# Logits of two softmax maps as six products in alternating row halves of TensorE, and the values' product in another PSUM bank

## The chip, the cores and the metric

The kernel runs on one core of one Trainium2 chip. The metric is device time in microseconds (us) of one launch, the median of several runs. Lower is better. A run's time is slightly longer than the span of its profile, which goes from the first to the last recorded instruction.

## The reference

A trunk of two layers over 1024 tokens of width 1024, in float32. Layer 0 mixes tokens with a gated MLP and a gated delta rule, layer 1 with differential attention. Each layer also has an MLP and a gated projection. The change lies in the attention of layer 1 alone, cut here to what matters:

```python
# 8 heads; q and k have two maps (r) of 64 columns per head, v has 128
q = rms_norm(q.reshape(1, 1024, 8, 2, 64), q_gain) * 64 ** -0.5
k = rms_norm(k.reshape(1, 1024, 8, 2, 64), k_gain)
# for each block of 128 query rows
logits = einsum('bqhrd,bkhrd->bhrqk', q_blk, k) - slopes * dist     # causal
probs = softmax(logits)
attn = probs[:, :, 0] - lam * probs[:, :, 1]
o = einsum('bhqk,bkhe->bqhe', attn, v)
```

Each logit is a sum over 64 numbers, and each head needs it for two maps.

## The kernel before

**Numbers as pairs.** Large products run in a rounded float32 format that streams faster. An operand is kept as a rounded high part and a low part that holds what rounding took away. A product of two such operands is high*high + high*low + low*high: three products added up in one PSUM bank (`mm3`, line 206).

**Logits.** For each head, `begin` (line 956) makes the keys' operand `ks`. For map r it is a tile of 128 partitions: the 64 partitions of the map's own half hold the high part of k, and the other 64 hold the low part. `put_k` transposes four tiles of k on TensorE into a PSUM tile with the tag `tr`, and per map one ScalarE instruction (L969) writes the high part and one VectorE instruction (L970) the low part. `put_q` does the same for two blocks of queries: `qh` has the high part of q in both halves (ScalarE L980, then a copy by VectorE, L981), and `ql` has the low part in the map's own half and zeros in the other (L982). So one product of 128 rows, `qh` against `ks`, gives high*high + high*low at once, and a second one, `ql` against `ks`, gives low*high. The logits of one map and one chunk of up to 512 keys are two products of 128 rows.

**A block's steps.** There are 64 blocks: 8 heads by 8 blocks of 128 queries. Block b sees (b+1)*128 keys, in one chunk (b below 4) or two. For each map and chunk `logits` runs the two products into a PSUM bank (tags `aux` and `sc`, in turns `aux, sc, aux`). VectorE then adds the distance term, writes the result to `lg` and keeps the running minimum (L1016). ScalarE takes the exponential and its sum (L1019). `combine` subtracts map 1 from map 0 (VectorE, L1025 to L1027). `transpose` turns the result with TensorE into `tr` banks, which ScalarE copies out (L1037). `value` multiplies by v into a bank with the tag `sc` (`po`), which VectorE (L1047) and ScalarE (L1049) read. Map 0 has three `lg` buffers, map 1 only one.

**PSUM.** There are eight banks: the tags `mm`, `tr`, `aux` and `sc`, with two buffers each.

**Order.** The loop over g at the end of `attention` writes the steps of three blocks interleaved: map 0's logits of block g, `combine` of g-1, `transpose` of g-2, map 1's logits of g, `value` of g-2. Between them `pump` issues filling work: the projections to q, k and v of later heads (`mm<-w,hi`, `mm<-w,lo`), and from the last heads on the output projection (`mm<-ohi,w`) with its transposes (`put_o`, L1073, L1074). A scheduler then fixes the order on each engine. An engine executes its own list in that order and waits where an operand or a buffer isn't ready. `Ordered` (line 44) wraps TensorE's calls; its `floor` puts an instruction behind a named one in that order without making the engine wait for it.

Of the kernel before, what the change touches and what calls it, by code (L numbers as in the profile page):

```python
# [12 lines left out]
F32R = mybir.dt.float32r  # L13
AF = mybir.ActivationFunctionType
ALU = mybir.AluOpType
# [3 lines left out]
P = 128  # L19
# [4 lines left out]
HT = 512  # L24
# [3 lines left out]
AHEAD = 7  # L28
WB = 12
EARLY = 3000  # L30
LAG = 3
KA = (6, 5)
MARKS = ((64, 50), (192, 144), (223, 168))
# [6 lines left out]
def f32(ap):  # L40
    return ap.bitcast(F32)
# [73 lines left out]
class Trunk:  # L115
# [756 lines left out]
    def attention(self, w_qkv, w_out, gain_next, h_dram):  # L872

        nc = self.nc
        NB = NT
        hs, r = list(self.hs), list(self.r)
# [75 lines left out]
        qk_tag = itertools.cycle(("aux", "sc", "aux"))  # L952
        aT_tag = itertools.cycle(("c8", "c9", "c10"))
        heads = {}

        def begin(hd):

            qk = qks[hd]

            ks = self.slot(f"A{2 + hd % 2}", [P, 2, S], F32R, "ks")  # L960

            def put_k(hf):
                pt = self.aux([P, HT], "tr", "tr")
                for t in range(4):
                    self.pe.transpose(pt[:, t * P : (t + 1) * P], qk[1][hf][:, t, :], self.ident)
                for r in range(2):
                    own, other = half[r], half[1 - r]
                    dst = ks[:, r, hf * HT : (hf + 1) * HT]
                    nc.scalar.activation(dst[own], pt[own], AF.Copy, scale=self.kg[own])  # L969
                    nc.vector.scalar_tensor_tensor(dst[other], pt[own], self.kg[own], f32(dst[own]), ALU.mult, ALU.subtract)  # L970

            def put_q(b2):
                pt = self.aux([P, HT], "tr", "tr")
                for i in range(2):
                    self.pe.transpose(pt[:, i * P : (i + 1) * P], qk[0][b2 // 2][:, 2 * (b2 % 2) + i, :], self.ident)
                qh = self.slot(f"c{11 + b2 % 2}", [P, 2, 2 * P], F32R, "qh")
                ql = qlow[b2 % 2]
                for r in range(2):
                    own, other = half[r], half[1 - r]
                    nc.scalar.activation(qh[own, r], pt[own, 0 : 2 * P], AF.Copy, scale=self.qg[own])  # L980
                    nc.vector.tensor_copy(qh[other, r], f32(qh[own, r]))  # L981
                    nc.vector.scalar_tensor_tensor(ql[own, r], pt[own, 0 : 2 * P], self.qg[own], f32(qh[own, r]), ALU.mult, ALU.subtract)  # L982
                return qh, ql

            put_k(0)
            heads[hd] = [ks, put_k, put_q, put_q(0)]

        class Block:
# [13 lines left out]
            def logits(me, r):  # L1002
                hd, b, n, nm, lg = me.hd, me.b, me.n, me.nm, me.lg[r]
                if b == 0 and r == 0:
                    nc.vector.tensor_scalar(al, al, 0.5, None, ALU.mult)
                ks, _, _, (qh, ql) = heads[hd][:4]
                qs = slice((b % 2) * P, (b % 2 + 1) * P)
                nch = (n + HT - 1) // HT
                u0 = (NB - 1 - b) * P
                for c in range(nch):  # L1010
                    k0, k1 = c * HT, min(n, (c + 1) * HT)
                    ps = self.aux([P, HT], next(qk_tag), "qk")
                    self.pe.matmul(ps[:, : k1 - k0], lhsT=qh[:, r, qs], rhs=ks[:, r, k0:k1], start=True, stop=False)
                    self.pe.matmul(ps[:, : k1 - k0], lhsT=ql[:, r, qs], rhs=ks[:, r, k0:k1], start=False, stop=True)

                    nc.vector.tensor_tensor_reduce(  # L1016
                        out=lg[:, k0:k1], in0=ps[:, : k1 - k0], in1=al[:, u0 + k0 : u0 + k1], scale=-1.0,
                        scalar=3.0e38 if c == 0 else nm[:, r, 0:1], op0=ALU.add, op1=ALU.min, accum_out=nm[:, r, c : c + 1])
                nc.scalar.activation(lg[:, :n], lg[:, :n], AF.Exp, bias=nm[:, r, nch - 1 : nch], scale=-1.0, accum_out=me.sums[:, b, r : r + 1])  # L1019

            def combine(me):
                b, n, sums = me.b, me.n, me.sums
# [16 lines left out]
            def value(me):  # L1039
                hd, b = me.hd, me.b  # L1040
                if b % 4 == 0:
                    os[hd].append(self.slot(f"c{6 + b // 4}", [P, 4, P], F32, "o"))
                o, v = os[hd], vs[hd // 2]
                po = self.aux([P, P], "sc", "po")
                for k in range(b + 1):
                    self.pe.matmul(po, lhsT=me.aT[k // 4][:, (k % 4) * P : (k % 4 + 1) * P], rhs=v[:, k, (hd % 2) * P : (hd % 2 + 1) * P], start=k == 0, stop=k == b)
                nc.vector.tensor_copy(o[b // 4][:, b % 4, :], po)  # L1047
                sq = self.tmp(P)
                nc.scalar.activation(sq, po, AF.Square, accum_out=me.osq[:, b : b + 1])  # L1049
# [81 lines left out]
        tail = tails()  # L1131
        blocks = []
        for g in range(8 * NB + 2):
            if g < 8 * NB:
                hd, b = divmod(g, NB)
                blocks.append(Block(hd, b))
                blocks[g].logits(0)
            if 0 < g <= 8 * NB:
                blocks[g - 1].combine()
            pump()  # L1140
            if g < 8 * NB and b % 2 and b < NB - 1:
                q = heads[hd][2]((b + 1) // 2)
            if g > 1:
                blocks[g - 2].transpose()
            pump()
            if g < 8 * NB:
                if b == 3 - (hd < 7):
                    heads[hd][1](1)
# [834 lines left out]
```

## Time and profile before

| | us |
|---|---|
| median of 3 runs | 2536.91 |
| lowest and highest run | 2536.68, 2537.27 |
| span of the profiled execution | 2535.2 |
| median run less that span (start and end around it) | 1.7 |
| attention's blocks: first to last logits product on TensorE | 1270.7 to 1720.4 |

Of the profiled execution the span is what is recorded; no separate run time stands beside it. In the profile PE is TensorE's products, PEld its weight loads, DVE VectorE, ACT ScalarE, POOL GpSimd. A TensorE row gives the start, the duration and the shape: `128*128` is rows by columns of the array in use, `128x512` is partitions by columns streamed. Successive products overlap, so a product's cost to TensorE is read from start to start and not from its duration. In merged timeline rows `x8` means that eight instructions start one after another, and the duration goes from the first start to the last end. A plain float32 product is recorded as two passes, a transpose or a rounded product as one.

### The profile page before, as it was taken

The page shows a single profiled execution, that of the slowest core. Times are in us where ns is not written, and L with a number is a line of the kernel's source. Part 1 is how long each engine was busy: PE and PEld are TensorE (multiplying, and loading weights), DVE is VectorE, ACT ScalarE, POOL GpSimd, SP SyncE. Part 2 cuts the span into 40 slices and gives each one's busy share as a digit, 9 for nine tenths or more (in the row PEclk, how much of TensorE's full clock was granted, in tenths as well). Part 3 has the DMA queues.
Part 4 walks back from the last instruction along what each step waited for, and adds up shares of the span by engine and source line. Part 5 has one row for each costly group of instructions (what it writes and reads, how often), then busy time and mean ns, then how long its engine had stood idle before and what let it go on. Part 6 is the DMA issues. An engine that isn't in the chain of part 4 may idle for free.

```text
span 2535.2 us, 40147 instructions
## 1 busy us (share of the span) xinstructions
PE 2515.3 (99%) x14046; PEld 2151.9 (85%) x14046; DVE 1854.3 (73%) x3676; ACT 1285.9 (51%) x2553; POOL 285.5 (11%) x256
## 2 busy tenths in 40 slices
PE   9999999999999999999999999999999999999999
PEld 7898898888888878888999999988778888888877
DVE  7867776697666888656477777787887677787586
ACT  6543444465455434544366666665654555445452
POOL 0301232000000000000334333310000000000000
PEclk9999999999999999999999999999999999999999
DMA  7452435457557756553211111147466558655651
GB/s 242 126 157 78 136 110 193 138 175 242 161 174 257 245 164 207 183 158 120 74 53 47 55 47 43 59 136 257 143 219 202 174 184 281 216 184 185 200 178 59
DMA packets 298818, 396.92 MB, mean 157 GB/s; under 512 B 37780, under 2 KB 165752, under 8 KB 298616
## 3 DMA queue, kind: packets, MB, share of 16 engines
q1 hardware_dynamic: 298600, 394.36, 48.4%
q8 instruction: 110, 1.80, 0.3%
q14 instruction: 92, 0.75, 0.1%
q10 hardware_dynamic: 16, 0.00, 0.0%
HBM read 289.40 MB, written 104.86 MB: 156 GB/s over the span
## 4 chain that ended last, share of the span: by engine, by line
PE 92%; DVE 4%; DMA 2%; issue 1%; ACT 1%; SPq 0%; POOL 0%; DVEq 0%; ACTq 0%; POOLq 0%
PE mm L76 79%; PE po L76 3%; PE qk L76 2%; PE aux L76 2%; PE tr L79 2%; DMA raw<-in_w_ple_gate_dram 1%; DVE lg L1016 0%; DVE w L224 0%; DMA raw<-in_w_mlp_dram 0%; PE pz L76 0%; PE py L76 0%; PE aux L79 0%; PE pvn L76 0%; PE pab L79 0%; PE pkq L76 0%
## 5 line engine op out<-in xcount | busy, mean ns | idle before, releaser
L76 PE MATMUL mm<-g,w 128*128 128x512 f32 x2592 | 603.6, 394 | 0.8 <-DVE g L224 0.5
L223 ACT CAST w<-raw 128x512 fp32r<-128x512 f32 x598 | 366.0, 618 | 453.8 <-PE mm L76 386.8
L76 PEld LDWEIGHTS mm<-g,w 128*128 128x128 f32 x2592 | 485.9, 188 | 116.2 <-DVE g L224 1.0
L76 PE MATMUL mm<-hi,w 128*128 128x512 f32 x1728 | 553.6, 396 | 0.3 <-ACT hi L1219 0.3
L76 PE MATMUL mm<-w,hi 128*128 128x256 f32 (+2 forms) x2528 | 505.5, 295 | 0.0
L224 DVE TENSOR_TENSOR w<-raw,w 128x512 fp32r<-128x512 f32 x534 | 364.8, 690 | 178.9 <-ACT w L223 169.4
L76 PEld LDWEIGHTS mm<-w,hi 128*128 128x128 f32 x2528 | 400.1, 188 | 13.6 <-DVE acc L284 0.3
L76 PEld LDWEIGHTS mm<-hi,w 128*128 128x128 f32 x1728 | 324.7, 188 | 73.7 <-ACT hi L1219 0.7
L76 PE MATMUL mm<-w,lo 128*128 128x256 f32 (+2 forms) x1264 | 370.3, 293 | 0.0
L76 PE MATMUL mm<-lo,w 128*128 128x512 f32 x864 | 341.6, 396 | 0.9 <-DVE lo L1220 0.9
L76 PE MATMUL mm<-t,w 128*128 128x512 f32 x1152 | 270.9, 394 | 1.2 <-ACT w L223 1.2
L76 PEld LDWEIGHTS mm<-t,w 128*128 128x128 f32 x1152 | 216.2, 188 | 52.8 <-ACT w L223 1.6
L76 PEld LDWEIGHTS mm<-w,lo 128*128 128x128 f32 x1264 | 238.2, 188 | 5.6
L76 PEld LDWEIGHTS mm<-lo,w 128*128 128x128 f32 x864 | 162.8, 188 | 36.8 <-DVE lo L1220 1.4
L224 DVE TENSOR_TENSOR g<-graw,g 128x512 fp32r<-128x512 f32 x216 | 147.2, 685 | 8.8 <-DMA gd<-g 6.9
L223 ACT CAST g<-graw 128x512 fp32r<-128x512 f32 x216 | 132.7, 617 | 32.8 <-issue 10.9
L1019 ACT ACTIVATE lg<-lg,nm 128x128 f32<-128x128 f32 (+7 forms) x128 | 99.5, 777 | 82.5 <-DVE nm L1016 76.0
L260 POOL TENSOR_TENSOR r<-ms,mhalf 128x4 f32<-128x4 f32 x12 | 13.3, 1109 | 1060.9 <-DVE ms L258 1033.5
L350 ACT ACTIVATE g<-g 128x512 f32<-128x512 f32 x96 | 60.6, 632 | 114.8 <-DVE g L284 114.5
L1016 DVE CUSTOM_DVE_ANT_0 lg<-qk,al 128x512 f32<-128x512 f32 (+3 forms) x128 | 75.1, 589 | 36.2 <-PE qk L76 32.8
L224 POOL TENSOR_TENSOR w<-raw,w 128x512 fp32r<-128x512 f32 x64 | 84.6, 1347 | 111.9 <-ACT w L223 63.0
L76 PE MATMUL mm<-ohi,w 128*128 128x512 f32 x256 | 85.2, 400 | 0.5 <-ACT ohi L1073 0.5
(336 smaller groups left out, 3612.4 us busy)
## 6 DMA issues: line engine op xcount, KB each, us to landing
raw<-in_w_mlp_dram SPq DMA_DIRECT2D x352, 256.0 KB, 3.3
graw<-gd SPq DMA_DIRECT2D x224, 256.0 KB, 2.8
gd<-g SPq DMA_DIRECT2D x192, 256.0 KB, 3.1
raw<-in_w_ple_gate_dram SPq DMA_DIRECT2D x76, 256.0 KB, 3.5
acc<-h_dram SPq DMA_DIRECT2D x64, 256.0 KB, 4.4
keep<-in_w_mlp_dram SPq DMA_DIRECT2D x64, 256.0 KB, 4.3
raw<-in_w_in_e_dram SPq DMA_DIRECT2D x60, 256.0 KB, 3.7
h_dram<-acc SPq DMA_DIRECT2D x48, 256.0 KB, 2.5
```

The source lines that it names most:

```text
L76: self._next(self.engine.matmul(*a, **k))
L79: self._next(self.engine.transpose(*a, **k))
L223: self.nc.scalar.copy(hi, src)
L224: (lo_engine or self.nc.vector).tensor_tensor(lo, src, f32(hi), ALU.subtract)
L260: nc.gpsimd.tensor_tensor(r, ms, self.mhalf[:, 0:4], ALU.pow)
L350: nc.scalar.activation(g, src, AF.Relu)
L1016: nc.vector.tensor_tensor_reduce(out=lg[:, k0:k1], in0=ps[:, : k1 - k0], in1=al[:, u0 + k0 : u0 + k1], scale=-1.0, scalar=3.0e38 if c == 0 ...
L1019: nc.scalar.activation(lg[:, :n], lg[:, :n], AF.Exp, bias=nm[:, r, nch - 1 : nch], scale=-1.0, accum_out=me.sums[:, b, r : r + 1])
```

## The change

The keys' operand `ks` becomes two tiles of 128 partitions, high and low, with map 0 in partitions 0 to 63 and map 1 in 64 to 127; the queries' operand has the same form. One ScalarE and one VectorE instruction over 128 partitions make each of them, where `put_k` had two and two and `put_q` two and four. The logits of both maps for one chunk are now made together: three products for each map, each of 64 rows and 128 columns, in the order map 0, map 1, map 0, map 1 and so on. Map 0 uses the array's upper 64 rows and writes an `aux` bank, map 1 the lower 64 rows and an `sc` bank. Each of the six is put behind the one before in TensorE's order, the first behind the exponential of an earlier chunk, and the scheduler gets a higher priority for them. `po` moves from `sc` to `tr`. In the loop `combine` of block g-1 now stands ahead of block g's logits, and both maps' logits stand together.

```diff
+AT_ONCE = 200
...
-        qlow = [self.slot(t, [P, 2, 2 * P], F32R, "ql") for t in ("c13", "d0")]
-        for t in qlow:
-            nc.vector.memset(f32(t), 0.0)
...
-                for r in range(2):
-                    own, other = half[r], half[1 - r]
-                    dst = ks[:, r, hf * HT : (hf + 1) * HT]
-                    nc.scalar.activation(dst[own], pt[own], AF.Copy, scale=self.kg[own])
-                    nc.vector.scalar_tensor_tensor(dst[other], pt[own], self.kg[own], f32(dst[own]), ALU.mult, ALU.subtract)
+                hi, lo = (ks[:, i, hf * HT : (hf + 1) * HT] for i in range(2))
+                nc.scalar.activation(hi, pt, AF.Copy, scale=self.kg)
+                nc.vector.scalar_tensor_tensor(lo, pt, self.kg, f32(hi), ALU.mult, ALU.subtract)
...
-                for r in range(2):
-                    own, other = half[r], half[1 - r]
-                    nc.scalar.activation(qh[own, r], pt[own, 0 : 2 * P], AF.Copy, scale=self.qg[own])
-                    nc.vector.tensor_copy(qh[other, r], f32(qh[own, r]))
-                    nc.vector.scalar_tensor_tensor(ql[own, r], pt[own, 0 : 2 * P], self.qg[own], f32(qh[own, r]), ALU.mult, ALU.subtract)
-                return qh, ql
+                q = self.slot(f"c{11 + b2 % 2}", [P, 2, 2 * P], F32R, "qs")
+                nc.scalar.activation(q[:, 0], pt[:, 0 : 2 * P], AF.Copy, scale=self.qg)
+                nc.vector.scalar_tensor_tensor(q[:, 1], pt[:, 0 : 2 * P], self.qg, f32(q[:, 0]), ALU.mult, ALU.subtract)
+                return q
...
-                    ps = self.aux([P, HT], next(qk_tag), "qk")
-                    self.pe.matmul(ps[:, : k1 - k0], lhsT=qh[:, r, qs], rhs=ks[:, r, k0:k1], start=True, stop=False)
-                    self.pe.matmul(ps[:, : k1 - k0], lhsT=ql[:, r, qs], rhs=ks[:, r, k0:k1], start=False, stop=True)
...
+                    pss = [self.aux([P, HT], t, "qk") for t in ("aux", "sc")]
+                    if len(scaled) > 1:
+                        self.pe.floor = scaled[-2]
+                    with self.tc.high_priority(AT_ONCE):
+                        for i, (x, y) in enumerate(((0, 0), (0, 1), (1, 0))):
+                            for r in range(2):
+                                self.pe.matmul(pss[r][:, : k1 - k0], lhsT=q[half[r], x, qs], rhs=ks[half[r], y, k0:k1], start=i == 0, stop=i == 2)
+                                self.pe.floor = self.pe.mark
+                    self.pe.floor = None
...
-                po = self.aux([P, P], "sc", "po")
+                po = self.aux([P, P], "tr", "po")
...
+            if 0 < g <= 8 * NB:
+                blocks[g - 1].combine()
             if g < 8 * NB:
                 hd, b = divmod(g, NB)
                 blocks.append(Block(hd, b))
-                blocks[g].logits(0)
-            if 0 < g <= 8 * NB:
-                blocks[g - 1].combine()
+                blocks[g].logits()
...
-                blocks[g].logits(1)
```

More of the change, by code (lines that the diff above doesn't have):

```diff
@@ L951, in attention @@
         lg1 = lgs[1][:, 1]
-        qk_tag = itertools.cycle(("aux", "sc", "aux"))
+        scaled = []
         aT_tag = itertools.cycle(("c8", "c9", "c10"))
@@ L1011, in logits @@
                     k0, k1 = c * HT, min(n, (c + 1) * HT)
-                    ps = self.aux([P, HT], next(qk_tag), "qk")
-                    self.pe.matmul(ps[:, : k1 - k0], lhsT=qh[:, r, qs], rhs=ks[:, r, k0:k1], start=True, stop=False)
-                    self.pe.matmul(ps[:, : k1 - k0], lhsT=ql[:, r, qs], rhs=ks[:, r, k0:k1], start=False, stop=True)
[L1016 to L1019, printed above, removed]
+                    pss = [self.aux([P, HT], t, "qk") for t in ("aux", "sc")]
[7 more added lines that the diff above has]
+                    self.pe.floor = None
+                    scaled.append(None)
+                    for r in range(2):
+                        nc.vector.tensor_tensor_reduce(
+                            out=lg[r][:, k0:k1], in0=pss[r][:, : k1 - k0], in1=al[:, u0 + k0 : u0 + k1], scale=-1.0,
+                            scalar=3.0e38 if c == 0 else nm[:, r, 0:1], op0=ALU.add, op1=ALU.min, accum_out=nm[:, r, c : c + 1])
+                for r in range(2):
+                    inst = nc.scalar.activation(lg[r][:, :n], lg[r][:, :n], AF.Exp, bias=nm[:, r, nch - 1 : nch], scale=-1.0, accum_out=me.sums[:, b, r : r + 1])
+                scaled[-nch:] = [inst.ins.name] * nch
             def combine(me):
```

15 lines of the change are left out of this document (6 added, 9 removed).

## The prediction

> **What bounds the kernel now.** First the page: span, busy time by engine, and the chain of work that ended last.
>
> ```profile
> span 2535.2 us, 40147 instructions
> PE 2515.3 (99%) x14046; PEld 2151.9 (85%) x14046; DVE 1854.3 (73%) x3676; ACT 1285.9 (51%) x2553; POOL 285.5 (11%) x256
> PE 92%; DVE 4%; DMA 2%; issue 1%; ACT 1%; SPq 0%; POOL 0%; DVEq 0%; ACTq 0%; POOLq 0%
> ```
>
> TensorE is busy for 99% of the span and carries 92% of the chain. As a busy TensorE need not be one at its peak, I look at the stage that changes: the windows of the attention, then what TensorE waited for in 1260 to 1760 us (total, times, longest).
>
> ```profile
> 1300.00:1400.00 100.00, 99.03 (x803) 96.72 (x802) 72.80 (x212) 62.08 (x153) 40.63 (x35) 1.00 0.17 51
> 1500.00:1600.00 100.00, 100.00 (x810) 97.89 (x810) 74.05 (x221) 61.41 (x153) 36.52 (x32) 1.00 0.14 43
> 1655.00:1720.00 65.00, 62.98 (x370) 53.65 (x369) 54.40 (x143) 40.52 (x95) 7.36 (x7) 1.00 0.47 153
> PE tr L79 <- DVE olo L1074: 1.8, 3, 0.7
> PE qk L76 <- DVE nm L1016: 1.5, 2, 0.8
> PE mm L76 <- ACT ohi L1073: 0.5, 1, 0.5
> PE po L76 <- ACT aT L1037: 0.4, 2, 0.2
> PE tr L79 <- ACT aT L1037: 0.2, 1, 0.2
> ```
>
> Of each 100 us TensorE (first pair after the length) is busy 99 to 100, VectorE (third) some 73, and the granted clock (the 1.00) is full. All waits of TensorE in these 500 us add up to 4.4 us. So the stage lasts as long as TensorE's own stream of products; only near 1655 to 1720 does VectorE, 54.4 of 65, come close. The change is worth what it does to that stream.
>
> **The products: three rounds for four.** The logits' products by tile, and their pace from the timeline:
>
> ```profile
> L76 PE MATMUL qk<-ks,qh x192: 219/392/483, 1270.7 to 1720.2; 128*128 128x512 f32 x96, 128*128 128x128 f32 x32, 128*128 128x256 f32 x32, 128*128 128x384 f32 x32
> L76 PE MATMUL qk<-ks,ql x192: 221/388/477, 1270.8 to 1720.4; 128*128 128x512 f32 x96, 128*128 128x128 f32 x32, 128*128 128x256 f32 x32, 128*128 128x384 f32 x32
> ...
> 1350.62 0.40 PE L76 MATMUL qk<-ks,qh 128*128 128x512 f32 x1
> 1350.85 0.39 PE L76 MATMUL qk<-ks,ql 128*128 128x512 f32 x1
> 1351.08 0.40 PE L76 MATMUL mm<-w,hi 128*128 128x256 f32 x2
> ...
> 1354.45 0.28 PE L76 MATMUL qk<-ks,qh 128*128 128x256 f32 x1
> 1354.57 0.28 PE L76 MATMUL qk<-ks,ql 128*128 128x256 f32 x1
> ...
> 1499.95 1.05 PE L76 MATMUL po<-v,aT 128*128 128x128 f32 x8
> ```
>
> From start to start 512 columns take 0.23 us and 256 take 0.12. For 384 I take the middle, 0.175. Eight passes of 128 columns start over 1.05 - 0.27 us, so 0.11 each: there the weight load of 128 columns sets the pace. I price a logits product of 128 columns at 0.11 too.
>
> Both maps of a chunk make a pair: 48 pairs of 512 columns (half of 96) and 16 each of 384, 256 and 128. One product per pair over all of them is 48 x 0.23 + 16 x (0.175 + 0.12 + 0.11) = 17.5 us. Before, a pair is four products one after another, 70 us in all. After, it is six in two halves of the array. If the halves run side by side these are three rounds, 52.5 us: **17.5 us saved**. That they run side by side is bounded by the nearest row, the delta rule's 32-row products, which go to different parts of the array:
>
> ```profile
> 200.10 0.45 PE L76 MATMUL pz<-inv 32*32 32x32 f32 x24
> 205.63 0.40 PE L76 MATMUL mm<-hi,w 128*128 128x512 f32 x1
> 205.96 0.67 PE L76 MATMUL py<-xt,am 64*64 64x64 f32 x8
> 206.57 0.51 PE L76 MATMUL mm<-hi,w 128*128 128x512 f32 x1
> 206.91 0.38 PE L76 MATMUL po<-state,qkv 128*128 128x128 f32 x2
> ...
> 205.96 0.54 PEld L76 LDWEIGHTS py<-xt,am 64*64 64x64 f32 x8 [0.36 <-issue]
> 206.56 0.19 PEld L76 LDWEIGHTS mm<-hi,w 128*128 128x128 f32 x1
> ...
> L76 PE MATMUL py<-xt,am x64: 218/218/267, 206.0 to 375.8; 64*64 64x64 f32 x64
> ...
> 4.27 0.18 PEld L79 LDWEIGHTS aux<-ident,t 8*128 8x128 f32 x1 [0.33 <-issue]
> 4.47 0.59 PEld L79 LDWEIGHTS aux<-ident,x 128*128 128x128 f32 x5
> ```
>
> 24 products of 32 columns last 0.45 us, the last one some 0.19 of it, so they start 0.011 apart. The 64-column ones, all in one part of the array, start (0.67 - 0.22)/7 = 0.064 apart, which would be 0.03 for 32 columns. So three parts do run side by side, loads included. No row shows two halves that share all 128 columns; that is the first rival.
>
> **The switch between array shapes.** The same rows show its price. The 512-column product at 205.63 would let the next start at 205.86; the first 64-row one starts at 205.96: 0.10 lost. Its load can't be made ahead: the first `py` lasts 267 ns instead of 218, 0.05 for 64 columns, so by the pace above 0.11 for 128. On the way back the last `py` starts at 205.96 + 0.67 - 0.22 = 206.41 and is paced out at 206.475, but the next load starts at 206.56: 0.09. That product's successor starts 0.34 after it instead of 0.23: 0.11 for its exposed load. Together **0.41 us per burst** of row-half products.
>
> Does a shape with half the rows but all columns pay this? The one instruction of that kind, 8 rows by 128 columns at 4.27, says yes: 0.11 for its load and almost nothing for its eight columns, and the next load should start at 4.38, but it starts at 4.47, again 0.09 later.
>
> How many bursts there are I read from the instruction order of the changed kernel. The 576 products stand in 61 uninterrupted runs: 37 of twelve, the others of two to eight. Before and behind them stand 128-row instructions. 61 x 0.41 = **25.0 us lost**.
>
> **The order inside a burst.** Each chunk's six products are chained, but where a burst holds two chunks A and B the scheduler interleaves the chains in 39 of the 61: map 0 A, map 1 A, map 0 B, map 0 A, map 1 B, map 1 A. Two neighbours then share a half, and as products start in their order, map 1's half lags by one product until the burst ends. By the shorter of the two chunks: 8 bursts at 0.23, 14 at 0.175, 8 at 0.12, 9 at 0.11 make 6.2 us, taken as **6 us lost**. Were the neighbours always in different halves it would be nothing.
>
> **VectorE and ScalarE.** Their rows in 1260 to 1760 us:
>
> ```profile
> L982 DVE SCALAR_TENSOR_TENSOR ql<-tr,qg,qh 64x256 fp32r<-64x256 f32 x64 | 30.9, 483 | 1.6
> L981 DVE CAST qh<-qh 64x256 fp32r<-64x256 f32 x64 | 26.0, 406 | 9.9 <-ACT qh L980 8.6
> L970 DVE SCALAR_TENSOR_TENSOR ks<-tr,kg,ks 64x512 fp32r<-64x512 f32 x32 | 24.0, 750 | 1.9 <-ACT ks L969 0.9
> L980 ACT ACTIVATE qh<-tr,qg 64x256 fp32r<-64x256 f32 x64 | 29.9, 467 | 22.0 <-PE tr L79 11.2 <-DVE ql L982 10.0
> L969 ACT ACTIVATE ks<-tr,kg 64x512 fp32r<-64x512 f32 x32 | 21.8, 682 | 9.7 <-PE tr L79 5.6 <-DVE ks L970 3.7
> ...
> L1016 DVE CUSTOM_DVE_ANT_0 lg<-qk,al 128x512 f32<-128x512 f32 (+3 forms) x128 | 75.1, 589 | 36.2 <-PE qk L76 32.8 <-PE tr L79 1.0
> L1016 DVE DVE_READ_ACCUMULATOR2_ANT nm<- 128x1 f32 x192 | 15.9, 83 | 0.0
> ...
> L1047 DVE COPY o<-po x64: 271/291/295, 1284.8 to 1743.3; 128x128 f32<-128x128 f32 x64
> L1049 ACT ACTIVATE t<-po x64: 257/278/286, 1285.2 to 1743.8; 128x128 f32<-128x128 f32 x64
> ```
>
> Twice the partitions at the same columns, for about the same time each: VectorE loses half of 30.9, all of 26.0 and half of 24.0, 53 us; ScalarE half of 29.9 and of 21.8, 26 us. All of it lies beside TensorE's products, and can give back at most the 4.4 us of waits above. The largest of them, on `olo`, is for work that stays. I take 0.
>
> The moved `combine` makes VectorE wait for block g-1's exponential with block g's reductions queued behind it. TensorE meets that only two chunks later, when it needs the same `aux` or `sc` buffer. The cover is the filling work: the median stretch between two bursts in the new order is some 36 instructions, 36 x 0.12 = 4.3 us, against the four reductions of a two-chunk block, 4 x (0.59 + 0.08) = 2.7 us. So 0, with the price without cover in the rivals. `po` in `tr` holds a transposes' bank for two readers, 0.29 + 0.28 us, while a second buffer is free and the same filling work runs: 0; uncovered, 0.57 in each of 64 blocks would be 36 us, which nothing in the new order suggests. No DMA moves.
>
> **The sum.** -17.5 + 25.0 + 6 = +13.5 us on the span of 2535.2. The median run is 1.7 us above that span, and I leave this as it is: 2536.9 + 13.5 = **2550 us**. With the waits between -4.4 and a few more, and the switch between 0.38 and 0.45, this case alone lies between 2541 and 2560.
>
> **The rivals.**
>
> *The halves do not run side by side* (they share all columns). Then six products replace four: +35 us, with the switches 25, no lag: 2597. For it: the products seen side by side differ in columns as well as rows. Against: their rows also overlap with nothing lost. In between, pairs may run at less than double pace, say half of the saving gone: +22, 2559; with all of it gone, 2568. The Trainium skill ("TensorE: Matmul & The Clock Gate", Measured speedup vs the span model) gives 3.07 for four row parts of 512 columns where four would be ideal; by that the rounds would cost 52.5/0.77 = 68 us, and an estimate by that page is 2566. No row here shows such a pair; the 32-row products come nearer to the ideal.
>
> *A wait takes the place of the products.* VectorE's four reductions now come together, and TensorE waits for a buffer. If a third of the bursts wait for one reduction, 20 x 0.67 = 13.5 us more: 2564. It decides where the filling work between two bursts is shorter than 2.7 us. For it: some stretches are of only two to four instructions. Against: those cut single chains and need no new buffer, and VectorE has 53 us less to do.
>
> *Faster: the switch is cheap between whole-column shapes*. If the next shape's weights can be loaded while the old products still run, neither the 0.19 of emptying nor the 0.22 of exposed loads is paid: -17.5 + 6 = -11.5, 2525. It decides below (17.5 - 6)/61 = 0.19 us per burst. For it: all measured switches but one also change the columns. Against: that one, at 4.27, lost the same 0.09. If only the emptying goes, 61 x 0.19 = 11.6 come back: +2, 2539.
>
> **How the numbers follow.** My sum 0.60. Not side by side 0.08 (2597), partly so 0.05 (2559 to 2568). Waits 0.12 (2564 and some more). Cheap switch 0.10 (2525), half cheap 0.05 (2539). About 0.2%, 5 us, can be told from no change. Faster by more is the cheap switch: 0.10. Within it are the half cheap switch and the lower end of my sum: 0.10. Slower is the rest: 0.80. The range from 2534 to 2574 leaves out the cheap switch and the serial case, 0.18.
>
> **What would show it.** In the profile after, `qk` rows of `64*128`, two starting together, pairs of 512 columns 0.23 apart; around each burst a gap of 0.09 to 0.10 beyond the pace and a first product longer by 0.11; about 61 such bursts; the attention's end some 13 us later, with TensorE's waits still a few us. It is wrong if pairs start 0.46 apart, if a 128-row load starts while row-half products still run, or if waits of TensorE on L1016 add up to over 10 us.

## The result: slower by 1.2%, and the profile after

The changed kernel takes 2568.6 us (median of 4 runs, 2566.3 to 2570.4) against 2536.8 us for the kernel before on the same chip (4 runs, 2536.5 to 2537.3). The ratio is 1.0123, with a 95% interval from 1.0109 to 1.0138. The forecast was 2550 us, slower by 13.5 us within 2534 to 2574. The direction and the range hold; the size does not: the loss is 31.8 us, more than twice the forecast.

In the code after, lines have moved a little: products are L77, transposes L80, the reductions of the logits L1014, exponentials L1018. The head of the page of the changed kernel, and its chain by engine:

```profile
span 2566.3 us, 40326 instructions
PE 2530.5 (99%) x14238; PEld 2144.1 (84%) x14238; DVE 1801.3 (70%) x3562; ACT 1254.8 (49%) x2505; POOL 287.9 (11%) x256
PE 92%; DVE 3%; DMA 2%; ACT 1%; issue 1%; POOL 1%; SPq 0%; DVEq 0%; ACTq 0%; POOLq 0%
```

VectorE lost 53.0 us of work (1854.3 to 1801.3; forecast 53) and ScalarE 31.1 (forecast 26), and yet the span grew by 31.1 us. TensorE is still busy for 99%. The loss shows in the windows of the attention (PE, PEld, VectorE, ScalarE and GpSimd busy with their counts, then the granted clock, DMA share and GB/s). The last two are stretches picked out below:

```profile
1300.00:1400.00 100.00, 94.88 (x788) 89.19 (x787) 60.54 (x180) 52.60 (x134) 38.17 (x31) 0.98 0.15 43
1500.00:1600.00 100.00, 99.31 (x850) 94.56 (x849) 56.91 (x186) 54.76 (x144) 38.68 (x33) 1.00 0.18 54
1655.00:1720.00 65.00, 59.02 (x374) 48.81 (x374) 43.81 (x123) 33.22 (x81) 10.27 (x9) 0.92 0.33 106
1381.30:1384.70 3.40, 3.40 (x17) 3.40 (x17) 2.94 (x4) 1.67 (x6) 2.35 (x3) 0.50 0.48 139
1678.20:1685.00 6.80, 5.53 (x20) 4.54 (x20) 4.82 (x10) 2.88 (x6) 1.64 (x1) 0.50 0.62 191
```

Before, TensorE was busy 99.03 of the first 100 us and 62.98 of the 65 near the end, at full clock throughout. Now 94.88 and 59.02, and parts of it at half clock. What TensorE waited for in 1250 to 1800 us (total, times, longest):

```profile
PE mm L77 <- DVE k L924: 7.6, 4, 3.7
PE qk L77 <- ACT qs L972: 3.1, 7, 1.1
PE mm L77 <- DVE t L1176: 2.3, 2, 1.2
PE tr L80 <- ACT aT L1037: 2.0, 2, 1.3
PE tr L80 <- DVE olo L1074: 1.9, 1, 1.9
PE po L77 <- ACT aT L1037: 1.4, 2, 0.7
```

The waits are on other things than forecast: not on the reductions (L1014, the forecast's L1016), but on the scaling of q and k that frees an `mm` bank (L924), on the queries' operand (L972), and on the copies behind transposes.

**An account of the 31.1 us of span.** From the raw TensorE rows between 1250 and 1850 us I took each start-to-start time, less the pace of that shape. What exceeds 0.25 us I count as a wait. The waits add up to 25.8 us, against 8.9 before: 16.9 more. (These sums are larger than those of the wait lists, which count a wait only from the modelled end of the last product.) Periods at half clock, of which the trace before has none in this stage, last 17.1 us; products in them take 8.1 us longer. The 61 bursts, without their waits, are a net loss of about 4 us (below). That is 29. The other 2 us lie ahead of the stage: up to 1250 us the same excess over the pace is some 1.9 us larger than before.

**One burst.** The timeline of TensorE around a burst of two chunks of 512 columns, and behind another burst that is followed by `mm` (a burst is a run of logits products with nothing else between them):

```profile
1372.43 0.28 PE L77 MATMUL mm<-w,hi 128*128 128x256 f32 x1
1372.64 1.66 PE L77 MATMUL qk<-ks,qs 64*128 64x512 f32 x12
1374.23 0.33 PE L80 MATMUL tr<-ident,lg 128*128 128x128 f32 x1
...
1430.57 0.33 PE L77 MATMUL qk<-ks,qs 64*128 64x384 f32 x2
1430.84 0.39 PE L77 MATMUL mm<-w,lo 128*128 128x256 f32 x1
1431.06 0.40 PE L77 MATMUL mm<-w,hi 128*128 128x256 f32 x2
...
L77 PE MATMUL qk<-ks,qs x576: 217/385/502, 1271.9 to 1745.8; 64*128 64x512 f32 x95, 64*128 64x128 f32 x37, 64*128 64x384 f32 x33, 64*128 64x256 f32 x27
```

Twelve products of 512 columns would take 12 x 0.23 = 2.8 us one after another. Here the next instruction starts 1.59 us after the first: six rounds of 0.231 are 1.39, the first load is 0.11, and the change back to the other shape is 0.09. So the halves do run side by side. The burst itself starts 0.21 behind a product of 256 columns that would let the next start after 0.12: 0.09. Behind the second burst, `mm` at 1430.84 has its successor after 0.22 instead of 0.12: an exposed load of 0.10.

Over all 61 bursts, waits taken out: in 0.09 each; the rounds longer by 0.11 for the first load (0.05 where the first chunk has 128 columns, whose pace is a load's anyway), less 0.05 for each round of 128 columns behind a longer one, and 0.05 more for a longer one behind it; out 0.09; the exposed load behind 0.10 before `mm` and `po` and 0.05 before transposes. In sum 5.6 + 5.4 + 6.1 + 4.5 = 21.6 us against the 17.5 saved.

**The longest wait.** TensorE, then VectorE in the same stretch without its short readouts (L1014's second instruction), then GpSimd:

```profile
1376.60 0.38 PE L77 MATMUL po<-v,aT 128*128 128x128 f32 x2
1376.82 0.60 PE L80 MATMUL tr<-ident,k 128*128 128x128 f32 x4
1381.11 0.68 PE L77 MATMUL mm<-w,hi 128*128 128x256 f32 x2 [3.69 <-DVE k L924]
1381.59 0.42 PE L77 MATMUL mm<-w,lo 128*128 128x256 f32 x1
1381.81 0.63 PE L77 MATMUL mm<-w,hi 128*128 128x256 f32 x2
```

```profile
1376.68 0.68 DVE L1014 CUSTOM_DVE_ANT_0 lg<-qk,al 128x512 f32<-128x512 f32 x1
1377.29 0.68 DVE L1014 CUSTOM_DVE_ANT_0 lg<-qk,al 128x512 f32<-128x512 f32 x1
1377.90 0.15 DVE L918 SCALAR_TENSOR_TENSOR ss<-ss,e 128x8 f32<-128x8 f32 x1
1377.98 0.74 DVE L1014 CUSTOM_DVE_ANT_0 lg<-qk,al,nm 128x512 f32<-128x512 f32 x1
1378.65 0.74 DVE L1014 CUSTOM_DVE_ANT_0 lg<-qk,al,nm 128x512 f32<-128x512 f32 x1
1379.43 0.69 DVE L996 TENSOR_SCALAR al<-al 128x1024 f32<-128x1024 f32 x1
1380.04 0.28 DVE L1047 COPY o<-po 128x128 f32<-128x128 f32 x1
...
1380.64 0.42 DVE L924 TENSOR_TENSOR k<-mm,ssf 128x256 f32<-128x256 f32 x1
...
1378.20 1.97 POOL L920 TENSOR_TENSOR ssf<-ss,mhalf 128x8 f32<-128x8 f32 x1 [0.35 <-DVE ss L918]
```

The order has the filling product behind `tr` of k, and both `mm` banks are full. One of them is freed by L924, which needs a chain VectorE, GpSimd, VectorE (L918, L920, then L924). L918 stood behind two of the burst's four reductions, and L924 behind the other two, the halving of `al` and a copy of `po`. So TensorE stands still from 1377.42 to 1381.11. Behind it, products of 256 columns start 0.21 to 0.22 apart instead of 0.12: the granted clock is 0.50 from 1381.3 to 1384.7.

### The profile page after: what moved, and what is told of

It reads as the page before. It is cut to its first block, busy times and chain, and to the rows that moved or that the text cites. A ratio compares the mean times of both kernels' runs of the same rounds, so it can differ in the third digit from the quotient of the medians.

```text
span 2566.3 us, 40326 instructions
## 1 busy us (share of the span) xinstructions
PE 2530.5 (99%) x14238; PEld 2144.1 (84%) x14238; DVE 1801.3 (70%) x3562; ACT 1254.8 (49%) x2505; POOL 287.9 (11%) x256
## 4 chain that ended last, share of the span: by engine, by line
PE 92%; DVE 3%; DMA 2%; ACT 1%; issue 1%; POOL 1%; SPq 0%; DVEq 0%; ACTq 0%; POOLq 0%
PE mm L77 79%; PE po L77 3%; PE aux L77 2%; PE tr L80 2%; PE qk L77 2%; DMA raw<-in_w_mlp_dram 0%; DVE w L225 0%; DMA t<-h_dram 0%; DMA acc<-h_dram 0%; ACT lg L1018 0%; PE pz L77 0%; PE py L77 0%; DVE lg L1014 0%; PE pvn L77 0%; PE aux L80 0%
## 5 line engine op out<-in xcount | busy, mean ns | idle before, releaser
L77 PE MATMUL mm<-g,w 128*128 128x512 f32 x2592 | 603.5, 394 | 1.3 <-DVE g L225 1.3
L77 PEld LDWEIGHTS mm<-g,w 128*128 128x128 f32 x2592 | 485.9, 188 | 116.5 <-DVE g L225 1.7
L77 PE MATMUL mm<-hi,w 128*128 128x512 f32 x1728 | 554.1, 396 | 0.3 <-ACT hi L1217 0.3
L77 PE MATMUL mm<-w,hi 128*128 128x256 f32 (+2 forms) x2528 | 506.6, 297 | 7.6 <-DVE k L924 7.6
L77 PEld LDWEIGHTS mm<-w,hi 128*128 128x128 f32 x2528 | 399.9, 189 | 19.9 <-DVE k L924 8.8
L77 PEld LDWEIGHTS mm<-hi,w 128*128 128x128 f32 x1728 | 324.7, 188 | 73.8 <-ACT hi L1217 0.7
L77 PE MATMUL mm<-w,lo 128*128 128x256 f32 (+2 forms) x1264 | 372.8, 295 | 0.0
L77 PE MATMUL mm<-lo,w 128*128 128x512 f32 x864 | 341.6, 396 | 0.9 <-DVE lo L1218 0.9
L77 PE MATMUL mm<-t,w 128*128 128x512 f32 x1152 | 270.9, 394 | 1.2 <-ACT w L224 1.2
L77 PEld LDWEIGHTS mm<-t,w 128*128 128x128 f32 x1152 | 216.2, 188 | 52.8 <-ACT w L224 1.6
L77 PEld LDWEIGHTS mm<-w,lo 128*128 128x128 f32 x1264 | 239.5, 190 | 6.1 <-issue 0.7
L77 PEld LDWEIGHTS mm<-lo,w 128*128 128x128 f32 x864 | 162.8, 188 | 36.8 <-DVE lo L1218 1.4
L1018 ACT ACTIVATE lg<-lg,nm 128x256 f32<-128x256 f32 (+7 forms) x128 | 99.2, 775 | 99.0 <-DVE nm L1014 98.8
L1014 DVE CUSTOM_DVE_ANT_0 lg<-qk,al 128x512 f32<-128x512 f32 (+3 forms) x128 | 72.5, 586 | 35.1 <-PE qk L77 32.0
L77 PE MATMUL mm<-ohi,w 128*128 128x512 f32 x256 | 87.0, 411 | 2.3 <-DVE t L1176 2.3
```

The costliest lines, as they stand in the source:

```text
L77: self._next(self.engine.matmul(*a, **k))
L1014: nc.vector.tensor_tensor_reduce(out=lg[r][:, k0:k1], in0=pss[r][:, : k1 - k0], in1=al[:, u0 + k0 : u0 + k1], scale=-1.0, scalar=3.0e38 if ...
L1018: inst = nc.scalar.activation(lg[r][:, :n], lg[r][:, :n], AF.Exp, bias=nm[:, r, nch - 1 : nch], scale=-1.0, accum_out=me.sums[:, b, r : r ...
```

## The experiments

Times are medians, each with its ratio to the kernel before on the same chip (2537.0 to 2537.7 us) and its 95% interval. "Waits" and "half" are the two terms of the account above, in the same stretch (8.9 and 0 us before, 25.8 and 8.1 after). No version that does all the work was faster than the kernel before.

**1. Is it the moved `combine`? (e1)** The changed kernel with `combine` of block g-1 between the two maps' reductions of block g.

```diff
+                    me.pss.append(pss)
+                me.reduce(0)
...
-            if 0 < g <= 8 * NB:
-                blocks[g - 1].combine()
...
+            if 0 < g <= 8 * NB:
+                blocks[g - 1].combine()
+            if g < 8 * NB:
+                blocks[g].reduce(1)
```

> As after, but map 0's reductions and exponential stand ahead of combine of the block before, as they did before the change, and only map 1's behind it; TensorE has the same 61 bursts. Theory M (VectorE waits at the moved combine with the reductions queued behind it, and TensorE pays): the waits fall, 2568 becomes some 2552. Theory B (the four reductions of a block come to VectorE in one bunch, whatever stands ahead of them, and hold up the work behind them): little changes, 2562 to 2572.

Measured: 2569.3 us, 1.0126 (1.0111 to 1.0141); waits 30.1, half 8.4. Of the two theories it is the second that held: the place of `combine` isn't the cause.

**2. `po` back in `sc`, the rest as changed (e2).**

```diff
-                po = self.aux([P, P], "tr", "po")
+                po = self.aux([P, P], "sc", "po")
```

> As after, but the values' product stays in the sc banks as before the change. In the new order of instructions the bursts are then cut: 121 in place of 61. By the price of a switch read from the trace after (0.09 in, 0.09 out, 0.05 to 0.11 for exposed loads on either side, some 0.33 us) 60 more bursts cost 20 us: 2588. If, instead, the waits of TensorE come from po holding the transposes' banks, 18 us of waits go and the two nearly cancel: 2570.

Measured: 2574.4 us, 1.0145 (1.0130 to 1.0160); waits 6.4, half 0. The waits are gone, and yet it is slower than the changed kernel. Logits and `po` now share `sc`, the scheduler tears the logits into 121 bursts, and many break a pair. By the same account of the rows these bursts cost 11.3 (in) + 21.3 (rounds) + 12.5 (out) + 11.8 (load behind) = 56.9 us against 17.5 saved: +39.4, less 2.5 us of waits, is 36.9, and 36.8 were measured. The time lies between the two forecasts. So `po` in `tr`, with the order that comes of it, keeps the bursts whole and brings the waits. One pays for the other.

**3. The same questions with products of 128 rows (e3, e8).** e3 is the changed kernel with the old operands and the old two products per map, so without any switch of shape. e8 is e3 with `po` in `sc`.

```diff
-                        for i, (x, y) in enumerate(((0, 0), (0, 1), (1, 0))):
+                        for i, x in enumerate((qh, ql)):
...
-                                self.pe.matmul(pss[r][:, : k1 - k0], lhsT=q[half[r], x, qs], rhs=ks[half[r], y, k0:k1], start=i == 0, stop=i == 2)
+                                self.pe.matmul(pss[r][:, : k1 - k0], lhsT=x[:, r, qs], rhs=ks[:, r, k0:k1], start=i == 0, stop=i == 1)
```

> The operands and the 128-row products of before (four for a pair of maps, no switch of the array's shape), in the order of the change: both maps' logits together and chained, combine ahead of them, po in the transposes' banks. Theory B or M (the order and the bunching cost the time): most of the loss stays, some 18 us of waits and some 6 to 8 us of half clock behind them, 2555 to 2565. Theory S (the row-half products and their switches cost the time, waits are only their shadow): 2537 plus or minus 5.

> As the run with the 128-row products in the order of the change (2601), with po back in sc. Theory P: the waits go, 2545 or less. Theory B: the bunch stays and with it most of the loss, 2580 to 2600.

Measured: e3, 2600.8 us, 1.0250 (1.0233 to 1.0267); waits 49.3, half 18.7. e8, 2546.3 us, 1.0033 (1.0021 to 1.0046); waits 13.5, half 3.0. e3 lies far above both of its forecasts; e8 is close to the one by which the waits go with `po`. So both maps together and the moved steps cost 9 us; `po` in `tr` on top of them costs 55. These 63 us have no row-half product in them. The changed kernel takes 32 us less than e3, which is not the worth of its products (17.5 saved, 21.6 paid): its waits and half clock are 34 us less. VectorE has some 50 us less work in it (1801.3 against 1851.4), and TensorE another order; which of the two made the difference isn't shown.

**4. Only the products (e4).** The kernel before with the new operands and three 64-row products per map and chunk, each map by itself in the old order.

```diff
-                    self.pe.matmul(ps[:, : k1 - k0], lhsT=qh[:, r, qs], rhs=ks[:, r, k0:k1], start=True, stop=False)
-                    self.pe.matmul(ps[:, : k1 - k0], lhsT=ql[:, r, qs], rhs=ks[:, r, k0:k1], start=False, stop=True)
+                    for i, (x, y) in enumerate(((0, 0), (0, 1), (1, 0))):
+                        self.pe.matmul(ps[:, : k1 - k0], lhsT=q[half[r], x, qs], rhs=ks[half[r], y, k0:k1], start=i == 0, stop=i == 2)
```

> The operands and the 64-row products of the change in the order of before: each map's three products by themselves, nothing side by side, po in sc. 157 bursts at 0.33 us are 52 us, and six products of a pair one after another are two rounds more than four, 35 us: 2537 + 87 = 2624 if the price per burst and the gain from side by side are as read; the order of before should bring no waits beyond its 4 us. If the order is not what brings the waits, 2640 and over.

Measured: 2624.4 us, 1.0341 (1.0325 to 1.0356); waits 1.2, half 0; 157 bursts. The forecast was 2624. The account gives 15.2 + 62.3 + 16.6 + 15.7 - 17.5 = +92.3, less 7.7 of waits: +84.6 against 86.8 measured. The price per burst holds where nothing else is in the way.

**5. Only `po` in `tr` (e7).** The kernel before with that one word changed.

> Before, with the values' product in the transposes' banks and nothing else. Theory P (po in tr brings the waits): TensorE waits 10 us or more in the attention and the clock falls to half behind the longest, 2550 to 2565. Theory B (the bunch of four reductions brings them): 2537 plus or minus 4.

Measured: 2579.0 us, 1.0161 (1.0146 to 1.0176); waits 33.2, half 7.2. The move that the prediction priced at nothing costs 41 us by itself, more than either theory gave. Of the 43.7 us of its span, added waits and half clock are 31.5; the rest is in delays of less than 0.25 us, and some 5 us of it lies outside the stage. Its waits in 1250 to 1800 us and an example:

```profile
PE tr L79 <- ACT t L1049: 5.8, 3, 3.7
PE tr L79 <- DVE ks L970: 4.8, 4, 1.7
PE qk L76 <- DVE qh L981: 3.9, 7, 1.1
...
1378.86 0.60 PE L79 MATMUL tr<-ident,k 128*128 128x128 f32 x4
1383.13 0.69 PE L79 MATMUL tr<-ident,q 128*128 128x128 f32 x2 [3.68 <-ACT t L1049]
```

The transposes of q are next on TensorE and need a `tr` bank. One holds k, the other `po`, whose second reader (L1049) ends the wait of 3.68 us. Before, `po` in `sc` could not hold them up.

**6. The order of the six products (e9).** The changed kernel with map 0's three products ahead of map 1's three.

```diff
-                        for i, (x, y) in enumerate(((0, 0), (0, 1), (1, 0))):
-                            for r in range(2):
+                        for r in range(2):
+                            for i, (x, y) in enumerate(((0, 0), (0, 1), (1, 0))):
```

> As after, but map 0's three products stand ahead of map 1's three, so that only the neighbours in the middle lie in different halves. If the halves run side by side only as neighbours in order, a pair takes five rounds for three, +35 us, and 18 more bursts at 0.33 us are +6: 2568 + 41 = 2609, less what the slower TensorE saves in waits, up to 20: 2590 to 2609. If a later product can pass a waiting one, the alternation is worth nothing: 2574.

Measured: 2586.6 us, 1.0190 (1.0175 to 1.0206); waits 18.1, half 1.9. The time lies between the two forecasts. The rounds are longer than ideal by 31.5 us instead of 5.4: alternating is worth some 26 us. Why, the timeline of this run shows:

```profile
1273.74 0.79 PE L77 MATMUL qk<-ks,qs 64*128 64x384 f32 x6
...
1276.90 0.97 PE L77 MATMUL qk<-ks,qs 64*128 64x512 f32 x6
...
1290.42 0.91 PE L77 MATMUL qk<-ks,qs 64*128 64x512 f32 x4
...
1291.58 1.24 PE L77 MATMUL qk<-ks,qs 64*128 64x512 f32 x8
```

Where the six stay together the order costs nothing. Six products of 512 columns in 0.97 are three rounds: 0.11 + 2 x 0.23 and some 0.39 for the last one, though in the order map 1's first one stands behind all three of map 0. What costs are bursts that the scheduler splits (79 bursts in place of 61). By the unmerged rows and TensorE's order, the third row is four products of map 0 alone (two of 512 columns, two of 128), with nothing beside them; the fourth has six of map 1 and only two of map 0. Two chunks with map 0's products ahead are cut in the middle; alternating ones are cut, if at all, between pairs.

**7. Which instruction holds the bank?** Five runs. Map 1's reductions put behind map 0's exponential in VectorE's order, so that four reductions don't stand in a row (e10); `po`'s square reading the copy in SBUF, so that `po`'s bank has one reader (e11 in the changed kernel, e13 in the kernel before with `po` in `tr`); `po` in `mm` on top of e10 (e12); and the copy of `po` at a higher priority on VectorE, in the kernel before with `po` in `tr` (e14).

```diff
+                        if r:
+                            self.pe.behind(red, inst.ins.name)
...
-                nc.scalar.activation(sq, po, AF.Square, accum_out=me.osq[:, b : b + 1])
+                nc.scalar.activation(sq, o[b // 4][:, b % 4, :], AF.Square, accum_out=me.osq[:, b : b + 1])
...
-                nc.vector.tensor_copy(o[b // 4][:, b % 4, :], po)
+                with self.tc.high_priority(200):
+                    nc.vector.tensor_copy(o[b // 4][:, b % 4, :], po)
```

> As after, but in the scheduler's order map 1's reductions come behind map 0's exponential, so that other work of VectorE can stand between the two maps' reductions. Theory B: the long waits of TensorE, which stand behind four reductions in a row, become short, the clock stays full, and some 15 us come back: 2550 to 2556. Theory P: 2563 to 2575.

> As after, but ScalarE squares the values' product from VectorE's copy in SBUF and not from PSUM, so that a transposes' bank is free again after one reader, L1047, and not after L1049 too. If the second reader holds the bank (theory P2), part of the 17 us of added waits goes: 2550 to 2560. If the first reader and the order do (theory P1), 2565 to 2572.

> As before with po in tr (2579), and ScalarE squares from VectorE's copy in SBUF. P2: the waits of the transposes on L1049 go, 5.8 us and the half clock behind them, 2560 to 2568. P1: 2574 to 2582.

> As the run with map 1's reductions behind map 0's exponential (2564), with the values' product in the projections' banks (mm) in place of the transposes' (tr); 63 bursts. If only tr is too scarce, the waits fall below 10 us: 2545 to 2552. If any shared pair of banks does the same, the projections wait instead and it stays at 2560 or above.

> The kernel before with po in the tag tr, as in the run that gave 2579.0 us, and with VectorE's copy of po (the first of its two readers) at a higher priority in the scheduler. First-reader theory: po's bank is held because that copy stands behind two or four reductions on VectorE, so the waits of 33 us shrink to below 20 and the time falls to 2555 to 2568. Rival, that any third user of the transposes' two banks shifts the whole order and its waits come wherever the order puts them: 2574 to 2584, waits of 28 us or more.

| run | us | ratio (95%) | waits | half |
|---|---|---|---|---|
| e10, map 1 behind | 2564.0 | 1.0102 (1.0087 to 1.0117) | 21.9 | 1.7 |
| e11, square from SBUF, after | 2565.8 | 1.0117 (1.0100 to 1.0134) | 23.6 | 6.4 |
| e13, square from SBUF, before | 2576.5 | 1.0155 (1.0140 to 1.0170) | 30.4 | 8.6 |
| e12, `po` in `mm` | 2570.5 | 1.0134 (1.0119 to 1.0149) | 29.5 | 3.7 |
| e14, copy at higher priority | 2581.4 | 1.0171 (1.0156 to 1.0186) | 33.6 | 11.7 |

e10 is a partial answer: waits on L924 fall from 7.6 to 2.3 us in its trace, the half clock from 8.1 to 1.7, and the time by only 4.6 us (2564.0 us, where the forecast for this cause was 2550 to 2556), as other waits grow. In its waits `olo` now stands first, with 3.8 us where the changed kernel had 1.9:

```profile
PE tr L80 <- DVE olo L1080: 3.8, 3, 2.1
PE qk L77 <- ACT qs L972: 2.8, 6, 1.1
PE mm L77 <- DVE k L924: 2.3, 3, 1.6
```

e11, e13 and e14 lie within 3 us of the kernels that they start from, and e12 6.5 us above e10. The theory that `po`'s second reader makes the waits, which the trace of e7 suggests so plainly, falls with e13: with that reader off the bank the waits end at other instructions. e14 does not test the first reader. In its trace the copy starts as late as in e7 (on average 0.50 us behind the end of `po`'s last product, at most 2.51; e7 0.47 and 2.49), and the second reader, here L1050, still ends the longest waits. Its time agrees with the rival by which any third user of the banks does it, but that the first reader plays no part isn't shown. The first waits of e13, then of e14:

```profile
PE qk L76 <- DVE qh L981: 6.4, 6, 1.5
PE mm L76 <- DVE k L923: 5.3, 5, 2.5
...
PE tr L79 <- ACT t L1050: 6.8, 3, 3.7
```

**8. How much is VectorE's load, and what is the change worth without it?** The subtraction of map 1 is left out of the changed kernel (e15) and of the kernel before (e16): map 0's numerators go on alone, and VectorE has some 70 us less to do.

> The changed kernel without the subtraction of map 1 (L1025 to L1027 left out: map 0's numerators go on alone), which takes some 58 us of work off VectorE and one step out of the chain from the exponential to the transposes; TensorE's instructions stay the same in kind and number. To be compared with the kernel before in the same form. If the waits come from VectorE's queue, most of the 25.8 us of waits and the half clock go, and this kernel lies 4 to 8 us above its partner (the bursts by the rows of the changed kernel), or 13 us by the prediction's prices. If the waits come from the order of TensorE's work alone they stay above 20 us and the difference stays 25 to 32 us.

> The kernel before without the subtraction of map 1, the partner of the run above. TensorE waits only some 9 us in the kernel before, so little can go: 2530 to 2538 us by either theory.

Measured: 2556.3 and 2533.5 us, apart by 22.8. Waits 20.0 and 5.7, half 1.6 and 0. The waits persist with an idler VectorE; the half clock mostly goes. Of the 22.8 us, 14.3 are waits and 1.6 half clock, which leaves 6.9 for the bursts and for what neither of the two covers: near the 4 of the account and half of the forecast's 13.5. The expectation for the partner (2530 to 2538) was met; the difference lies between the two theories, nearer to the one of the order.

**9. Is it the order's filling work?** In TensorE's order before, the filling between attention steps comes in small pieces: 17 stretches have 20 or more products. After, 52 have. Here each piece is tied behind the attention's last instruction of two pump steps earlier, in the kernel before with `po` in `tr` (e17), in the changed kernel (e18), and in the kernel before alone, as a control (e19).

```diff
+            self.pe.slot()
+            self.pe.fill = True
...
+            self.pe.fill = False
...
+        self.pe.start(2)
...
+        self.pe.start(0)
```

> The kernel before with po in the tag tr (2579.0 us in an earlier run), and with each piece of filling work put in TensorE's order behind the attention's last instruction of two pump steps earlier (a limit on how far ahead filling may run, no wait). By the instruction order, filling stretches of 20 and more instructions between the logits fall from 38 (931 instructions) to 16 (400); the kernel before has 17 (436). Theory, the waits come from how unevenly the order lays out the filling: waits fall from 33 us to below 15 and the time to 2540 to 2558. Rival, po's place in the transposes' banks itself makes the waits: 2570 to 2585.

> The changed kernel with the filling tied in the same way: its long filling stretches fall from 52 (1303 instructions) to 29 (701), the 61 bursts stay. Theory of uneven filling: waits and half clock shrink by about half, 25 + 8 to some 15, so 2568.6 becomes 2550 to 2558. Rival, the banks: 2564 to 2575.

> Control: the kernel before with the filling tied in the same way (long stretches 13 instead of 17). By either theory no change: 2533 to 2542 us. If it is slower by more, the tie itself costs and the two runs beside it have to be read against this one.

Measured: 2586.9 us, 1.0200 (1.0185 to 1.0216); 2578.4 us, 1.0169 (1.0151 to 1.0186); 2567.6 us, 1.0123 (1.0108 to 1.0138). All three lie above every forecast made for them. The waits of e17 are 39.5 us and those of e18 30.1, more than without the tie (33.2 and 25.8), with some 16 and 9 us of half clock. The control decides: it has the kernel before's instructions and banks, fewer long stretches (13), and waits of 29.1 and half clock of 8.6. So the length of the filling stretches is not the measure of it, and the theory falls. But the control shows something else. A change of order alone, with nothing in another bank, costs 30 us. Its waits in 1250 to 1800 us:

```profile
PE tr L79 <- ACT aT L1037: 5.5, 6, 1.4
PE tr L79 <- issue: 3.9, 2, 2.2
PE tr L79 <- DVE ks L970: 3.6, 5, 1.0
PE qk L76 <- DVE nm L1016: 3.2, 5, 1.1
```

There is no single culprit here: these are many short waits. I read each as work that the order has put too close ahead of its user, but no run tests that.

## Why the prediction was wrong in size

**Right: the bound, the sign, the rounds.** TensorE has 92% of the chain before and after, and with 84 us of work taken off VectorE and ScalarE the span still grew. (That this work was worth nothing isn't shown: e3, which keeps it, waits 49.3 us and not 25.8.) The halves run side by side at the full pace, so the rival of shared columns is out. The number of bursts was 61, as read from the order.

**Burst prices: somewhat too dear.** In and out were right (0.10 and 0.09 forecast, 0.09 and 0.09 measured). The first load costs 0.11 as forecast in most bursts and 0.05 in some; the load behind costs 0.05, not 0.11, where transposes follow; and rounds of 128 columns behind longer ones take 0.06 and not 0.11. **The lag of interleaved chains, put at 6 us, is nothing.** That step said "as products start in their order, map 1's half lags by one product". They don't start in their order: each half has its own succession. In the raw rows a product of map 1 starts beside its partner, ahead of one of map 0 that stands before it in the order and waits for its own half. So TensorE's part is about +4 (at most +6.9 by e15 and e16) and not +13.5.

**Wrong: the waits, put at nothing.** The step that failed is the cover: "the same filling work runs: 0; uncovered, 0.57 in each of 64 blocks would be 36 us, which nothing in the new order suggests". In its place the runs show 16.9 us of added waits and 8.1 of half clock. By itself that move, with the order that comes of it, costs 41 us (e7), and 55 with both maps together and 128-row products (e3 against e8). The cover was reckoned as a median, 36 instructions between two bursts, against the length of one queue of four reductions. A median doesn't cover the stretches where the filling stands elsewhere, and a reader's delay is not its own duration: it is all that stands ahead of it, here two reductions at a time and, for L924, a chain over VectorE and GpSimd. That `mm` banks, on which the filling depends, would be the ones held up was not considered: the forecast's place for the waits, L1016, was wrong. So was its assumption that a different order has as few waits as the old one. e19 shows that even before's own work waits 29 us in another order.

**Missing: the half clock.** 8.1 us behind the waits. No row before could have priced it in this stage, since no wait listed there exceeded 0.9 us.

Of the rivals, the one of waits (2564, "and some more") has the mechanism, with a chance of 0.12 and with the wrong buffers. The one of halves that share columns gives 2568 with the saving all gone; that this is the measured time is luck, as the rounds ran at the full double pace. The range held because it was drawn for these rivals, and not by the sum, whose terms, as measured, come to +4 of the 31.8.

**What stays open.** That waits and the half clock behind them make the loss is shown, and that moving `po` is enough to bring them; which property of TensorE's order makes them isn't settled. Kernels with `po` in `sc` waited 1.2 to 13.5 us, save the tied control; all with it elsewhere 18.1 us or more. Both the bank and the order change in each of those, since the scheduler's order follows from the banks. `po` in `tr` under exactly the order of before was not tried.

## What to carry to other kernels

This kernel's bounding engine, busy for 99%, owes that to an order that fits (e19), and a change of buffers or of grouping makes a new order. Here the waits of a new order were up to 49 us, instructions saved or not, so they are to be priced before the products are. A cover is counted at its thinnest places, and for every buffer on the way of the filling work itself. Products in different row halves do double the pace, but each visit to another shape costs about 0.35 us around it (21.6 us in 61 bursts). A burst of one chunk of 512 columns saves 0.23, one of two such chunks 0.46: only the longer visit pays, and only with both halves in it.

## What the runs showed of the hardware

**The clock falls behind some 2 us of idleness within 3.4 us.** In the changed kernel half clock followed four times. A second example, whose half clock lies at 1442.70 to 1446.10:

```profile
1439.68 0.60 PE L80 MATMUL tr<-ident,k 128*128 128x128 f32 x4
1443.15 0.58 PE L77 MATMUL mm<-w,hi 128*128 128x256 f32 x1 [2.87 <-DVE k L924]
...
1442.70:1446.10 3.40, 2.95 (x14) 0.50 0.62 178
```

In this trace each half-clock period lasts 3.413 us or twice that, and their starts (1381.262, 1442.702, 1678.222, 1715.768) lie whole multiples of 3.413 us apart, 18, 69 and 11. In the 3.413 us ahead of each, TensorE was idle for 3.3, 2.4, 1.9 and 2.1 us; where it was idle for 1.24 or less at full clock, the clock stayed full. So two waits of 1.1 us in one such window (1712.4 to 1715.8) had the same effect as one of 2. The Trainium skill ("TensorE: Matmul & The Clock Gate", Part 1: The HAM clock gate) has such a free-running window of 3413 ns and a half rate behind an idle one. The trace agrees in the length and the rate, but here a window idle for little more than half of it was enough. No sharp limit comes out of all the traces between 1200 and 1850 us: of the windows at full clock, every one idle for more than 1.89 us (e17) had half clock behind it, and of those idle for less than 1.28 (e14) only one had, of 0.78 in e9.

**The two halves of the array run like two queues.** In the unmerged rows behind the second line of e9 above, map 1's first product starts 0.01 us after map 0's first and ahead of map 0's second and third, which stand before it in the order. In longer bursts of that run map 1's first product, sixth in the order, starts only with map 0's second: it passes three waiting ones there and not four. The Trainium skill ("TensorE: Matmul & The Clock Gate", Step-by-step: what each phase is for) has products in program order, with only weight loads pulled ahead. Across two row halves these rows show otherwise.

**A change to a shape with half the rows costs as much as one that also has half the columns:** 0.09 us in and 0.09 out, in 61 bursts, for `64*128` against `128*128`, where the prediction's rows have 0.10 and 0.09 for `64*64`.
